# First chunk of x as float32 rows on the hardware queues, with w's first quarter behind them

## The chip, the cores and the metric

The kernel runs on one core of one Trainium2 chip. The metric is device time in microseconds of one execution. Time before: a median of 904.07 us over three runs (903.53 to 904.18).

## What is computed

```python
B, S, D = (16, 2048, 1024)          # x: (B, S, D), w: (D, D), decay: (D), all float32
xw = x @ w
out[:, 0, :] = xw[:, 0, :]
for t in range(1, S):
    out[:, t, :] = decay[None, :] * out[:, t - 1, :] + xw[:, t, :]
```

So it is one large matrix product and, along the time axis, a decayed running sum for each of the 1024 output columns.

## The kernel before, in words

The tokens are cut into 64 chunks of 512 (`TL`). The product is made transposed: weights stand still in TensorE as 64 tiles of 128 by 128 (`wsb`, index k for the eight slices of the inner dimension, n for the eight groups of output columns), and a chunk's tokens stream past as 512 columns. So x must arrive with its inner dimension on the partitions. In the steady state GpSimd's DMA queue loads a chunk with conversion to bf16 into `xb` (`load`, L105), one DMA for each quarter of the partitions ("quad"), VectorE transposes it in blocks of 32 (`turn`, L115, into `xw`), and a copy splits even and odd slices (`part`, L123, into `xt`). The other engines then form the running sums of each output group and store them through SP's queue (L306).

Everything that is issued is pinned: each engine executes its own instructions, DMA issues included, in the order in which the program text makes them. The table `agenda` writes that order out as letters; its entry -99 is the opening of the kernel, which is all that the change touches. The letters in it:

- `U0` to `U3` (`load_part`, L323): four DMAs each, a quarter of w: U0 is output half 0, even slices; U1 half 0, odd slices; U2 and U3 the same for half 1. They land in `stage` and are copied into `wsb` by `W`/`w` (`settle`, L330, VectorE/ScalarE; index 0 to 3 belongs to U0, 4 to 7 to U1, 8 to 11 to U2, 12 to 15 to U3) and by `q4`, `Q4` (L419).
- `M1`, `M2`, `M3` (`load_half`): four DMAs each for half a chunk of x: M1 is the second half of chunk 0, M2 and M3 are chunk 1.
- `I1`: GpSimd makes the bf16 identity `eye`.
- The first half of chunk 0 (256 tokens) goes another way: two DMAs (L341), one on SP's queue and one on ScalarE's, bring 128 float32 rows each. `H` (VectorE) and `J` (ScalarE) are `gather`, which converts and reorders rows (L376); `t` is `erect`, which transposes on TensorE against `eye` (L386); `O` (ScalarE) and `o` (VectorE) are `lay`, which copies the transposed block from PSUM into `xt` (L393). `gather`'s index i takes rows u = i mod 2, where u = 1 are the rows that ScalarE's queue brought.
- `K` (`spin_on`): ScalarE copies one column of a landed quad of U0 into a `gate` tile (L404), and two or three matmuls on that gate, whose result nobody reads, keep TensorE going. Twelve such matmuls on zeros (`spin`, L352) run at the very start.
- `E`, `F`, `G`: `turn` and `part` for one quarter of half a chunk (E4 to E7: second half of chunk 0; E8 to E15: chunk 1).
- `n` (`begin`): the first real matmuls, k even, n = 0 to 3, for the first (n0) and the second (n1) 256 tokens of chunk 0. After the agenda's opening, step 0 issues k odd for chunk 0, then chunk 1 in two halves. That finishes the first four output groups of two chunks.

ScalarE also issues DMAs: those of its own queue stand in its instruction order. Before the agenda it issues its one row DMA, then a copy called `touch` (L344). SP issues its row DMA and, after the spins, four small DMAs for `decay` (L356).

Of the kernel before, what the change touches and what calls it, by code (L numbers as in the profile page):

```python
# [9 lines left out]
FP32 = mybir.dt.float32  # L10
BF16 = mybir.dt.bfloat16
# [3 lines left out]
def _ap(ap_obj: bass.AP, new_ap, extra_offset=0):  # L15
    return dataclasses.replace(
        ap_obj,
        ap=[list(p) for p in new_ap],
        offset=ap_obj.offset + extra_offset,
    )  # L20
# [5 lines left out]
def kernel(  # L26
# [26 lines left out]
    nc = tc.nc  # L53
    pin = tc.keep_in_program_order
    B, S, D = x.shape
    assert w.shape == (D, D)

    NQ = 4
    P = 32
    CQ = D // NQ  # L60
    K = CQ // P
    M = K // 2
    TL = 512
    NJ = TL // P
    NC = S // TL
    R = K // 2
    CH = D // 2
    CR = CH // NQ

    const = ctx.enter_context(tc.tile_pool(name="const", bufs=1))  # L70
    sb = ctx.enter_context(tc.tile_pool(name="sb", bufs=1))
# [4 lines left out]
    def ring(pool, name, count, shape, dtype=FP32):  # L76
        i = turns[name] = turns.get(name, -1) + 1
        return pool.tile(shape, dtype, name=f"{name}{i % count}")

    def quad(q):  # L80
        return slice(q * P, (q + 1) * P)
# [12 lines left out]
    def ot_tile(nj):  # L94
        return ring(sb, "ot", 4, [128, nj, CR])

    xb_of = {}
    xw_of = {}
    xt_of = {}
# [25 lines left out]
    def matmul(ps, n, k, xt, t0=0, t1=TL, start=0, pairs=None):  # L125
        if pairs is None:
            rhs = xt[:, k // 2, k % 2, t0:t1]
        else:
            rhs = pairs[:, k // 2, t0 // P:t1 // P, :, k % 2].rearrange("p j i -> p (j i)")
        lhs = wsb[:, k, n].rearrange("p q i -> p (q i)")  # L130
        pin(nc.tensor.matmul(  # L131
            out=ps[:, t0:t1] if ps.shape[1] >= t1 else ps,
            lhsT=lhs,
            rhs=rhs,
            start=(k == 0 and t0 == start),
            stop=(k == K - 1),
        ))
# [3 lines left out]
    class Tile:  # L141
# [39 lines left out]
        def copy(self):  # L181
            self.xs = sb.tile([128, 2 * TL], FP32, name=f"xs{self.lot % 3}")[:, 0:self.T]
            parts = self.ps if isinstance(self.ps, tuple) else (self.ps,)
            size = self.T // len(parts)
            for i, ps in enumerate(parts):
                pin(nc.scalar.copy(out=self.xs[:, i * size:(i + 1) * size], in_=ps))  # L186
# [103 lines left out]
    class Outlet:  # L290
# [8 lines left out]
        def store(self, b, t0, j0, j1):  # L299
# [4 lines left out]
            for j in range(j0, j1, nj):  # L304
# [8 lines left out]

    room = [ot_tile(2 * NJ).rearrange("p j c -> p (j c)") for _ in range(2)]
    size = M * CH
    stage = {(0, 0): room[0][:, 0:size // 2].bitcast(BF16),
             (0, 1): room[0][:, size:size * 3 // 2].bitcast(BF16),
             (1, 0): room[1][:, 0:size // 2].bitcast(BF16),
             (1, 1): room[1][:, size // 2:size].bitcast(BF16)}

    def load_w(queues, h, e):
        for i, q in enumerate((0, 2, 1, 3)):
            pin(queues[i % len(queues)].dma_start(  # L323
                out=stage[h, e][quad(q)].rearrange("p (m d) -> p m d", m=M),
                in_=_ap(w, [[2 * D, P], [2 * P * D, M], [1, CH]],
                        (q * CQ + e) * D + h * CH)))

    def settle(h, e, m, copy):
        src = stage[h, e][:, m * CH:(m + 1) * CH]
# [3 lines left out]
    idle = const.tile([128, TL], BF16, name="idle")  # L333
    spare = ring(psp, "spare", 1, [128, TL])
    rows = const.tile([128, 2, P], FP32, name="rows")
    touch = const.tile([128, 1], BF16, name="touch")
    H = NJ // 2
    halves = ((0, H), (H, NJ))
    whole = room[1][:, size:2 * size].rearrange("p (u c) -> p u c", u=2)
    for u, queue in enumerate((nc.sync, nc.scalar)):  # L340
        pin(queue.dma_start(out=whole[:, u], in_=_ap(x, [[D, 128], [1, D]], u * 128 * D)))  # L341
    pin(nc.vector.memset(idle, 0.0))  # L342
    pin(nc.vector.memset(rows, 0.0))
    pin(nc.scalar.copy(out=touch, in_=idle[:, 0:1]))  # L344

    gates = [const.tile([128, 128], BF16, name=f"gate{q}") for q in range(NQ)]
    for gate in gates:
        pin(nc.vector.memset(gate, 0.0))

    def spin(count, by):  # L350
        for _ in range(count):
            pin(nc.tensor.matmul(out=spare, lhsT=by, rhs=idle, start=True, stop=True))  # L352

    spin(12, idle[:, 0:128])
    for q in range(NQ):
        pin(nc.sync.dma_start(  # L356
            out=rows[q * P:q * P + R],
            in_=_ap(decay, [[P, R], [CH, 2], [1, P]], q * CR)))
    cols = const.tile([128, 2, P], FP32, name="cols")

    def load_half(i):
# [5 lines left out]
    firsts = [ps[:, 0:TL] for ps in heads] + [spares[0]]  # L367
    seconds = [ps[:, TL:2 * TL] for ps in heads] + [spares[1]]
    eye = const.tile([128, 128], BF16, name="eye")

    upright = room[0][:, size * 3 // 2:2 * size].bitcast(BF16).rearrange(
        "p (e u m c) -> p e u m c", e=2, u=2, m=M)

    def gather(i, copy):
        e, u = i // 2, i % 2
        pin(copy(out=upright[:, e, u].rearrange("p m (q i) -> p m q i", q=NQ),  # L376
                 in_=whole[:, u].rearrange(
                     "p (q m i e) -> p e m q i", q=NQ, m=M, e=2)[:, e]))

    def bed(e):  # L380
        return seconds[e].bitcast(BF16).rearrange("p (m t) -> p m t", m=M)

    def erect(i):
        e, u = i // 2, i % 2
        for m in range(M):
            pin(nc.tensor.transpose(  # L386
                out=bed(e)[:, m, u * 128:(u + 1) * 128], in_=upright[:, e, u, m], identity=eye))

    def lay(i, copy):
        e, m = i // 2, i % 2 * 2  # L390
        if 0 not in xt_of:
            xt_of[0] = ring(sb, "xt", 5, [128, M, 2, TL], BF16)
        pin(copy(out=xt_of[0][:, m:m + 2, e, 0:H * P], in_=bed(e)[:, m:m + 2]))  # L393

    def begin(i):
        for k in range(0, K, 2):
            for n in range(R):
                if i == 0:
                    matmul(firsts[n], n, k, xt_of[0], 0, H * P)
                else:  # L400
                    matmul(firsts[n], n, k, xt_of[0], H * P, TL, pairs=xw_of[0])

    def spin_on(q):
        pin(nc.scalar.copy(out=gates[q][quad(q), 0:1], in_=stage[0, 0][quad(q), 0:1]))  # L404
        spin(3 if q == 0 else 2, gates[q])

    def load_part(i):
        load_w((nc.gpsimd,), i // 2, i % 2)

    def part_one(i, copy):  # L410
        part(i // 8, copy, i % 4, i % 4 + 1, *halves[i // 4 % 2])
# [106 lines left out]
    def turn_and_load(c):  # L518
# [16 lines left out]
        "w": lambda i: settle_one(i, nc.scalar.copy),  # L535
        "M": load_half,
        "U": load_part,
        "E": lambda i: turn(i // 8, *halves[i // 4 % 2], i % 4, i % 4 + 1),
        "F": lambda i: part_one(i, nc.vector.tensor_copy),
        "G": lambda i: part_one(i, nc.scalar.copy),  # L540
        "K": spin_on,
        "t": erect,
        "H": lambda i: gather(i, nc.vector.tensor_copy),
        "J": lambda i: gather(i, nc.scalar.copy),
        "O": lambda i: lay(i, nc.scalar.copy),
        "o": lambda i: lay(i, nc.vector.tensor_copy),
        "n": begin,
        "q": lambda i: settle_slots(i, 0, 1),
        "Q": lambda i: settle_slots(i, 1, R),
# [19 lines left out]
        "L": lambda i: load(*loads.pop(0)) if loads else None,  # L569
    }  # L570
    agenda = {
        -99: "U0 I1 M1 U1 M2 M3 U2 U3 H0 J1 t0 t1 H2 J3 t2 t3 O1 o0 K0 O3 o2 K2 K1 K3 W0 W1 w2 W3 n0 E4 E5 G4 E6 G5 E7 F6 G7 n1 q4 w5 Q4 W6 W7 D E8 E9 G8 E10 G9 E11 F10 G11 E12 L E13 G12 L E14 G13 E15 L F14 G15",
        0: "p0 z0 W8 W9 W10 W11",
        1: "g0",
        2: "L S1 L",
# [88 lines left out]
    for step, (g, n) in enumerate(slots):  # L664
        T = TL * len(g)
        left = step - len(slots)
        if n % R == 0:
            ns, nj = range(n, n + R), T // P
            if left == -2 * R:
                outlets = [Outlet(ns, H, half) for half in range(2)]  # L670
            else:
# [4 lines left out]
        if step == 0:  # L676
# [3 lines left out]
            for k0 in range(0, K, 2):  # L680
                for i in range(R):
                    for k in (k0, k0 + 1):
                        matmul(seconds[i], i, k, xt_of[1], 0, H * P,
                               pairs=xw_of[1] if k0 < 4 else None)
            for i in range(R):
                for k in range(K):
                    matmul(seconds[i], i, k, xt_of[1], H * P, TL, H * P,
                           pairs=xw_of[1] if i < 2 else None)
        if step < R:
            ps = heads[n] if n < 3 else tuple(spares)  # L690
        else:
# [16 lines left out]
            elif step == K:  # L708
                todo = []
                nexts = (ring(psp, "spare", 1, [128, TL]), ring(psp, "ps", 3, [128, TL]))  # L710
                for l in range(len(g)):
                    for i, half in enumerate((ps[:, l * TL:(l + 1) * TL], nexts[l])):
                        for k in range(K):
                            matmul(half, n + i, k, xt_of.get(g[l]),
                                   pairs=xw_of[g[l]] if g[l] in (3,) else None)
# [51 lines left out]
```

## Time and profile before

| what | value |
|---|---|
| median of three runs | 904.07 us |
| the profiled execution | 903.72 us, of which the span of the trace is 901.9 us |
| TensorE (PE) busy | 891.2 us, 99% of the span |
| VectorE (DVE), ScalarE (ACT), GpSimd (POOL) busy | 91%, 76%, 73% |
| first real matmul starts | 9.95 us |
| first group of four output blocks done, next one starts | 25.55 us |
| mean granted TensorE clock | 1.000 of full speed |

Times in a profile line are in microseconds from the start of the span: first the start, then the duration, the engine, the source line, what is written from what, and how many instructions were merged into the row; in brackets the idle time of that engine before the row and what ended it. ACTq and SPq are DMA issues of ScalarE and SyncE.

### The profile page before, as it was taken

To read this page: it belongs to the slowest core of one execution; us is meant where nothing else is said; L and a number is where in the kernel's file an instruction comes from. 1 tells how busy PE (TensorE), PEld (TensorE's weight loads), DVE (VectorE), ACT (ScalarE), POOL (GpSimd) and SP (SyncE) were. 2 spreads that over 40 slices of the span, in tenths; PEclk is the share of its full clock that TensorE was granted. 3 is DMA by queue.
4 is the path that set the end of the run, shared out by engine and by line. 5 is a ranking of instruction groups with operands and counts; after the bars stand their busy time and mean duration, and the time that the engine had idled before them with its cause. 6 is when DMAs were issued, how large, how long until landed. Compare 5 with 4: busy or idle time off the path is not lost.

```text
span 901.9 us, 12229 instructions
## 1 busy us (share of the span) xinstructions
PE 891.2 (99%) x4131; PEld 411.9 (46%) x4213; DVE 823.5 (91%) x636; ACT 687.1 (76%) x962; POOL 657.2 (73%) x757
## 2 busy tenths in 40 slices
PE   8999999999999999999999999999999999999998
PEld 5544444444444444444444444444444444444444
DVE  4999998989999999999998999999999999999998
ACT  4889867778877877878778778777787787787743
POOL 8888678768767768677677687777777776876532
PEclk9999999999999999999999999999999999999999
DMA  9999999999999999999999999999999999999868
GB/s 193 195 215 218 229 212 207 216 233 247 247 248 255 248 255 252 246 254 250 222 235 228 218 236 227 233 226 227 232 230 227 227 236 222 226 228 221 177 153 231
DMA packets 402382, 204.77 MB, mean 227 GB/s; under 512 B 9360, under 2 KB 401552, under 8 KB 402320
## 3 DMA queue, kind: packets, MB, share of 16 engines
q1 hardware_dynamic: 265664, 134.77, 60.8%
q0 software_dynamic: 136512, 68.70, 56.8%
q8 instruction: 33, 0.54, 0.2%
q10 hardware_dynamic: 144, 0.52, 0.1%
q14 instruction: 29, 0.24, 0.1%
HBM read 138.42 MB, written 134.22 MB: 302 GB/s over the span
## 4 chain that ended last, share of the span: by engine, by line
PE 97%; DMA 1%; issue 1%; POOL 0%; DVE 0%; ACT 0%; DVEq 0%; POOLq 0%
PE ps L131 96%; PE spare L131 1%; DMA ot<-in_w_dram 1%; POOL ot L323 0%; DVE so L233 0%; PE ps L460 0%; PE spare L460 0%; ACT xb L467 0%; DVE wsb L419 0%; DVEq L419 0%; POOLq L751 0%
## 5 line engine op out<-in xcount | busy, mean ns | idle before, releaser
L131 PE MATMUL ps<-xt,wsb 128*128 128x512 bf16 (+1 forms) x3946 | 862.6, 378 | 4.7 <-DVE wsb L419 0.4
L131 PEld LDWEIGHTS <-wsb 128*128 128x128 bf16 x4160 | 406.5, 98 | 479.8 <-issue 0.9
L208 POOL TENSOR_TENSOR xs<-h,xs 128x512 f32<-128x512 f32 (+1 forms) x190 | 242.7, 1278 | 184.1 <-ACT h L169 83.1
L283 DVE STREAM_TRANSPOSE ot<-so 128x1024 f32<-128x1024 f32 (+2 forms) x265 | 300.2, 1171 | 6.5 <-DMA out_dram<-ot 4.4
L186 ACT COPY xs<-ps 128x1024 f32<-128x1024 f32 (+1 forms) x190 | 188.8, 994 | 149.3 <-PE ps L131 137.5
L266 POOL TENSOR_TENSOR so<-h,xs 128x512 f32<-128x512 f32 (+1 forms) x190 | 241.2, 1271 | 46.9 <-ACT h L169 27.2
L123 ACT COPY xt<-xw 128x2048 bf16<-128x2048 bf16 (+1 forms) x133 | 240.6, 1816 | 9.5 <-DVE xw L115 9.5
L105 POOL DMA_DIRECT2D xb<-in_x_dram x260 | 171.6, 661 | 2.9 <-DMA ot<-in_w_dram 0.9
L169 ACT ACTIVATE h<-so,dec 128x512 f32<-128x512 f32 (+1 forms) x190 | 145.3, 766 | 32.8 <-DVE so L213 29.9
L115 DVE STREAM_TRANSPOSE xw<-xb 128x2048 f32<-128x2048 f32 (+1 forms) x74 | 145.9, 1981 | 6.5 <-DMA xb<-in_x_dram 6.5
L213 DVE TENSOR_TENSOR_SCAN so<-spare,keep,xs 128x512 f32<-128x512 f32 (+1 forms) x97 | 119.8, 1237 | 25.9 <-POOL xs L208 25.6
L213 DVE TENSOR_TENSOR_SCAN so<-spare,xs 128x512 f32<-128x512 f32 x93 | 113.0, 1217 | 25.4 <-POOL xs L208 22.8
L169 ACT ACTIVATE h<-ps,dec 128x512 f32<-128x512 f32 (+1 forms) x189 | 129.3, 684 | 0.0
L233 DVE TENSOR_TENSOR_SCAN so<-dec,ps 128x1024 f32<-128x1024 f32 x34 | 76.9, 2260 | 0.8 <-ACT h L169 0.6
L233 DVE TENSOR_TENSOR_SCAN so<-dec,keep,ps 128x1024 f32<-128x1024 f32 (+2 forms) x35 | 74.7, 2138 | 0.0
L270 ACT COPY keep<-so 128x1 f32<-128x1 f32 x136 | 25.2, 188 | 9.1 <-DVE so L233 8.7
L204 ACT COPY so<-keep 128x1 f32<-128x1 f32 x97 | 18.4, 191 | 2.6 <-DVE ot L283 2.4
L131 PE MATMUL spare<-xt,wsb 128*128 128x512 bf16 (+1 forms) x68 | 14.0, 329 | 0.0
L323 POOL DMA_DIRECT2D ot<-in_w_dram x16 | 9.0, 561 | 2.9 <-POOLq L751 0.9
L202 POOL MEMSET so<- 128x1 f32 x93 | 10.7, 116 | 0.6 <-DVE ot L283 0.6
L131 PE MATMUL ps<-xw,wsb 128*128 128x256 bf16 (+1 forms) x56 | 9.3, 307 | 0.8 <-DVE xw L115 0.8
L352 PE MATMUL spare<-idle 128*128 128x512 bf16 x12 | 5.3, 632 | 1.2 <-DVE idle L342 1.2
(46 smaller groups left out, 43.9 us busy)
## 6 DMA issues: line engine op xcount, KB each, us to landing
out_dram<-ot SPq DMA_DIRECT2D x236, 512.0 KB, 10.8
xb<-in_x_dram POOLq DMA_DIRECT2D x248, 256.0 KB, 7.8
out_dram<-ot SPq DMA_DIRECT2D x56, 128.0 KB, 2.5
ot<-in_w_dram POOLq DMA_DIRECT2D x16, 128.0 KB, 5.6
out_dram<-ot SPq DMA_DIRECT2D x8, 256.0 KB, 4.2
xb<-in_x_dram POOLq DMA_DIRECT2D x12, 128.0 KB, 5.3
out_dram<-xb SPq DMA_DIRECT2D x4, 256.0 KB
ot<-in_x_dram ACTq DMA_DIRECT2D x1, 512.0 KB, 4.9
```

The lines of the kernel that those rows point to most:

```text
L105: pin(nc.gpsimd.dma_start(out=xb_of[c][quad(q), j0:j1], in_=_ap(x, [[D, P], [P * D, j1 - j0], [1, CQ]], (b * S + t0 + j0 * P) * D + q * CQ)))
L115: pin(nc.vector.transpose(out=dst.rearrange("p (m j i) -> p j m i", m=M, i=P)[:, j0:j1, m0:m1], in_=src.rearrange("p (j m c) -> p j m c", ...
L123: pin(copy(out=xt_of[c][:, m0:m1, :, j0 * P:j1 * P], in_=src))
L131: pin(nc.tensor.matmul(out=ps[:, t0:t1] if ps.shape[1] >= t1 else ps, lhsT=lhs, rhs=rhs, start=(k == 0 and t0 == start), stop=(k == K - 1),))
L169: pin(nc.scalar.activation(out=h, in_=src, func=mybir.ActivationFunctionType.Copy, scale=dec[:, self.n:self.n + 1]))
L186: pin(nc.scalar.copy(out=self.xs[:, i * size:(i + 1) * size], in_=ps))
L208: pin(nc.gpsimd.tensor_tensor(out=odds, in0=self.g, in1=odds, op=ALU.add))
L213: pin(nc.vector.tensor_tensor_scan(out=so[:, 3:T + 2:2], data0=squares[-1][:, n:n + 1].to_broadcast([128, T // 2]), data1=self.xs[:, 1:T:2 ...
L233: pin(nc.vector.tensor_tensor_scan(out=so[:, t + 2:t + 2 + size], data0=dec[:, n:n + 1].to_broadcast([128, size]), data1=ps, initial=befor ...
L266: pin(nc.gpsimd.tensor_tensor(out=self.so[:, 2:T + 2:2], in0=self.h, in1=self.xs[:, 0:T:2], op=ALU.add))
L270: pin(nc.scalar.copy(out=self.keep, in_=self.so[:, self.T + 1:self.T + 2]))
L283: pin(nc.vector.transpose(out=outlet.ot[:, j:j + size, c0:c0 + P], in_=self.so[:, t1:t1 + size * P].rearrange("p (i t) -> p i t", t=P)))
```

## The change

The second 256 tokens of chunk 0 also come as float32 rows, two more DMAs on SP's and ScalarE's queues, and take the way over `gather`, `erect` and `lay`. w's first quarter (before: U0 on GpSimd, converted on the way) now comes as float32 behind those rows, cut in two along the slices m and by quads: SP takes quads 0 and 2, ScalarE quads 1 and 3, two DMAs each per cut. In program order that makes six DMAs on SP (then the four of `decay`) and six on ScalarE, where `load_rest(nc.scalar, 1)`, five DMAs, stands after `touch` and before every gather. GpSimd no longer issues U0 and M1; it first makes `eye`, then executes `hold`, a copy of one column of the first 256 rows, so that it waits for them, and then issues U1, M2, M3, U2, U3. The gates go; `K5` and `K1` are plain spins of five and one. `begin` runs 512 columns at a time, one k per letter. The staging for the new rows is `xb`'s buffer of chunk 0, and the converted rows stand in `xw`'s.

```diff
-    def load_w(queues, h, e):
-        for i, q in enumerate((0, 2, 1, 3)):
-            pin(queues[i % len(queues)].dma_start(
...
+    def load_w(queue, h, e, m0=0, m1=M, quads=range(NQ)):
+        for q in quads:
+            pin(queue.dma_start(
...
-    for u, queue in enumerate((nc.sync, nc.scalar)):
-        pin(queue.dma_start(out=whole[:, u], in_=_ap(x, [[D, 128], [1, D]], u * 128 * D)))
+    def load_rest(queue, u):
+        load_rows(queue, 1, u)
+        for m0, m1 in ((0, 2), (2, M)):
+            load_w(queue, 0, 0, m0, m1, (u, u + 2))
+
+    load_rows(nc.sync, 0, 0)
+    load_rows(nc.scalar, 0, 1)
+    load_rest(nc.sync, 0)
     pin(nc.vector.memset(idle, 0.0))
     pin(nc.vector.memset(rows, 0.0))
     pin(nc.scalar.copy(out=touch, in_=idle[:, 0:1]))
...
+    load_rest(nc.scalar, 1)
...
     def begin(i):
-        for k in range(0, K, 2):
-            for n in range(R):
-                if i == 0:
-                    matmul(firsts[n], n, k, xt_of[0], 0, H * P)
-                else:
-                    matmul(firsts[n], n, k, xt_of[0], H * P, TL, pairs=xw_of[0])
...
+        for n in range(R):
+            matmul(firsts[n], n, 2 * i, xt_of[0])
+
+    def hold(i):
+        pin(nc.gpsimd.tensor_copy(out=held, in_=wholes[0][:, :, 0:1].rearrange("p u c -> p (u c)")))
...
-        -99: "U0 I1 M1 U1 M2 M3 U2 U3 H0 J1 t0 t1 H2 J3 t2 t3 O1 o0 K0 O3 o2 K2 K1 K3 W0 W1 w2 W3 n0 E4 E5 G4 E6 G5 E7 F6 G7 n1 q4 w5 Q4 W6 W7 D E8 ...",
+        -99: "I1 v U1 M2 M3 U2 U3 H0 J1 t0 t1 H2 J3 t2 t3 O1 o0 O3 o2 K5 H4 J5 t4 t5 H6 J7 t6 t7 o4 O5 K1 W0 n0 o6 w1 n1 W2 O7 n2 W3 n3 q4 w5 Q4 W6 W7 D E8 ...",
```

## The prediction

> **What bounds the kernel now.** I read the chain of waits on the page first, then TensorE's rows of the timeline, then the rows of the other engines for the first 28 us, then the chain of that stretch.
>
> ```profile
> PE 97%; DMA 1%; issue 1%; POOL 0%; DVE 0%; ACT 0%; DVEq 0%; POOLq 0%
> ```
>
> That is the chain of the whole span; these are TensorE's own rows of the timeline:
>
> ```profile
> 9.95 0.49 PE L131 MATMUL ps<-xt,wsb 128*128 128x256 bf16 x3
> ...
> 12.62 0.51 PE L131 MATMUL ps<-xw,wsb 128*128 128x256 bf16 x3 [0.76 <-DVE xw L115]
> ...
> 14.97 0.82 PE L131 MATMUL ps<-xt,wsb 128*128 128x512 bf16 x2 [0.37 <-DVE wsb L419]
> ...
> 25.55 14.66 PE L131 MATMUL ps<-xt,wsb 128*128 128x512 bf16 x65
> ```
>
> From 14.97 us TensorE runs without a hole to the tail, so whatever moves the end of the first group (25.55) moves the end of the kernel by as much. A 512-column matmul is issued every 0.216 us, a 256-column one every 0.109 us. The first group is 16 x 0.216 (n0 and n1 together) + 10.45 (step 0, measured from 14.97, with 0.13 of slack) = 13.9 us; from 9.95 that would end at 23.9. The other 1.7 us are the two holes before 12.62 and 14.97 (waits for the second half of chunk 0, then for U1). So a perfect opening that starts at S ends the group at S + 13.9, and breaks even at S = 11.65.
>
> **What the change does to S if all goes as drawn.** ScalarE and the DMA queues:
>
> ```profile
> 0.74 0.41 ACTq L341 DMA_DIRECT2D ot<-in_x_dram  x1
> 0.75 0.39 SPq L341 DMA_DIRECT2D ot<-in_x_dram  x1
> ...
> 5.43 0.80 DVE L376 CAST ot<-ot 128x512 bf16<-128x512 f32 x2 [3.92 <-DMA ot<-in_x_dram]
> 5.65 1.21 ACT L376 CAST ot<-ot 128x512 bf16<-128x512 f32 x2 [2.98 <-DMA ot<-in_x_dram]
> 7.23 0.58 ACT L393 COPY xt<-ps 128x512 bf16<-128x512 bf16 x1 [0.37 <-PE ps L386]
> ...
> 7.84 0.98 DVE L393 COPY xt<-ps 128x512 bf16<-128x512 bf16 x2 [1.62 <-ACT xt L393]
> ```
>
> The DMA view of the first 26 us shows 365 to 416 GB/s while both queues bring rows; 1.05 MB more take 2.6 us, so rows 256 to 511 land near 8.1, w's first half (0.52 MB) near 9.4, the second near 10.7. H4 stands behind o2, though, and o0 and o2 wait for ScalarE's O1 and O3 (last row: done at 8.82). So H4 (0.40) ends near 9.2, H6 at 9.6, the transposes of H4 and J5 (0.22 for four at full clock) near 9.8, o4 (0.49) near 10.4, W0 from float32 (0.40, like the cast) near 10.8: S = 10.8. w1, W2 and W3 then stay ahead of 0.86 us of matmuls per k. U1, now behind `hold`, has the queue from about 5.9; the 4.2 MB up to its end land near 13.3 at that rate, its copies end before n3 does (14.25). End 10.8 + 13.9 = 24.7, a gain of 0.85 us: 903.2.
>
> Sizes off the path: GpSimd loses eight issues (2.32 + 2.41) and waits until 5.7 instead; behind `hold` are U1, M2, M3, U2, U3 and all later loads. M2 (VectorE took it at 17.49) follows the same 5 MB as before and is needed 0.6 us before step 0's second part, M3 (20.21) later still, U2 (23.75) at the end of the group; none is late here, and less so if S is late. VectorE loses 1.42 + 0.38, gains 0.80 + 0.98; ScalarE loses 1.66 + 0.80, gains 1.21 + 1.15; SP has nothing else to do until 38.45. Those are cover, not path; without it the largest of them is 0.98.
>
> **The step that I think decides.** ScalarE now issues five more DMAs, and its first cast J1 stands behind them in its order. An issue alone is cheap (0.41, so 2.67 + 5 x 0.41 = 4.7, before 5.65). But an issue can wait. On GpSimd it does:
>
> ```profile
> 1.31 1.25 POOL ot L323 x2
> 2.56 5.65 DMA ot<-in_w_dram
> 8.21 0.28 issue
> 8.50 0.54 POOL ot L323
> ```
>
> This is the chain of the opening. The third DMA is issued at 2.56 and lands at 8.21; the eleventh, eight later, is issued 0.28 us after that. The records of the trace name the semaphore of each DMA: eight on GpSimd (99 to 106), in turn, and each issue waits for the landing of the DMA eight before it. The hardware queues' records, in order of time:
>
> ```
> 0.74 ACT  semaphore=107          38.45 SP  semaphore=117
> 0.75 SP   semaphore=109          38.82 SP  semaphore=118
> 1.24 SP   semaphore=112          39.44 SP  $S[107]>= semaphore=107
> 1.62 .. 2.26 SP  113, 114, 115   45.16 SP  $S[109]>= semaphore=109
> ```
>
> Eight again, shared by SP and ScalarE: the ninth DMA takes 107, which was ScalarE's, and waits for it. Before, only six are issued in the opening and nothing is felt. The change has sixteen. In program order: rows 0 (SP), rows 1 (ScalarE), five of SP, five of ScalarE, four of decay. ScalarE's last four are the ninth to twelfth: they wait for rows 0 (5.4), rows 1 (5.6), SP's second rows (8.1) and SP's first piece of w. That last landing: two pieces of 131 KB in parallel take 0.65 us at 405 GB/s; at the rate at which GpSimd's quads land (131 KB each 0.66 us) 1.3 us. So 8.7 to 9.4; I take 9.1, the middle, since quads 0 and 1 share their stretch with GpSimd's U1. With the issue's 0.4, J1 starts at 9.5 instead of 5.65. If records are given out in another order than the program's (107 went to ScalarE, though SP's row stands first), decay or ScalarE come earlier or later; the last of ScalarE's five then waits for something that lands between 5.6 and 9.4.
>
> From J1 on the chain is the same as drawn above, where J1 at 5.65 gave 10.8: J1, J3, O1, O3 on ScalarE, then o2, H4, H6, o4, W0 on VectorE. So n0 starts at J1 + 5.15 = 14.65. By then w, U1 and M2 have landed, and w1, W2, W3, q4, W6 are ahead of the matmuls. End of the group 14.65 + 13.9 = 28.55: **+3.0 us**. Bounds: J1 at 8.4 (ScalarE waits only for SP's second rows) gives +1.9; J1 at 10, with the rest of ScalarE's chain stretched by 0.5, gives +4.0.
>
> The sum against the profiled execution: span 901.9 + 3.0 = 904.9, with 1.8 us around it 906.7. That execution (903.72) lay 0.35 below the median, to which I add: 904.07 + 3.0 = 907.1.
>
> **Rivals.**
> 1. *The issues don't hold ScalarE up* (the semaphores fall so that ScalarE's wait for the first rows at most, or are already passed): S = 10.8, 903.2. For it: nothing before shows ScalarE held by an issue. Against: the wait is in the records of SP and GpSimd alike. The point that decides: break-even is J1 = 6.5 (11.65 - 5.15), so a wait beyond the first rows' landing turns the gain into a loss.
> 2. *Not held up, but w lands slowly*: its pieces go to 32 partitions each, as GpSimd's quads do, and those never exceed some 200 GB/s written. Then 1.05 MB take 5.3 us from 8.1: W2 at 13.9, n2 and n3 end near 15.9, the group at 26.3, +0.8: 904.8. Against: those quads are converted, so 400 GB/s are read at that rate, and either side could be the limit. [...]
> 3. *Held up, and the clock falls.* TensorE then has nothing from about 6.7 (t0) to 10.2 (t1):
>
> ```profile
> 1.20 5.30 PE L352 MATMUL spare<-idle 128*128 128x512 bf16 x12 [1.20 <-DVE idle L342]
> ```
>
> and by stretches of the tail (length, busy time of the five engines, then PEclk, DMA share, GB/s):
>
> ```profile
> 901.00:902.00 1.00, 0.00 (x0) 0.00 (x0) 0.00 (x0) 0.00 (x0) 0.00 (x0) 0.59 0.00 0
> ```
>
> The early spins take 0.43 us each, twice the later 0.216; and in the last microsecond, some 3 us after the last matmul, the granted clock (0.59) goes down. A pause of 3.5 us may do the same here: K5 then takes 2.1 instead of 1.1 and holds t4 back by 0.8, t4 and t5 cost 0.4 more, and n0 to n3, if still slow, up to 3.4. I take +1.2 to +3.4 on top: 908.3 to 910.5. [...]
>
> **How the numbers follow.** Held up at full clock 0.46, held up with the clock down 0.24, as drawn 0.20, slow w 0.10. A measurement of this kernel tells about 0.2%, 1.8 us. Slower by more than that takes J1 past 8.3: nearly all of the first two, 0.65. Within: the last two and the early end of the first, 0.32. A gain of 1.8 would need S = 9.85, before o4 has ended: 0.03. The likeliest case's own range is 906.0 to 908.1; that of 8 in 10 reaches down to the case as drawn and up into the slow clock: 903.0 to 909.5.
>
> **What would show it.** Right: in the timeline ScalarE's issues between 2.7 and 9, with gaps, J1 near 9.5 with the DMA named before it; `hold` near 5.7 on GpSimd; t0 alone on TensorE before 7 and t1 after 10; n0 near 14.6 with no holes after; the 512-column row of step 4 starting near 28.5. Clock: K5's spins at 0.43 each. Wrong: J1 at 5.65 and n0 near 10.8 (then rival 1; with W2 waiting for a DMA, rival 2), or holes in TensorE after n3, which would mean that GpSimd's late start is felt after all.

## The result, and the profile after

The changed kernel takes **906.54 us** (median of seven runs, 906.25 to 907.19), the kernel before 903.66 (903.53 to 904.18) beside it: 2.9 us more, a ratio of 1.0031 (95% interval 1.002 to 1.0043). The profiled execution of the changed kernel took 907.0, with a span of 905.2; before it was 903.72 with 901.9.

The chain of waits still belongs to TensorE:

```profile
PE 98%; DMA 1%; ACT 0%; DVE 0%; ACTq 0%; issue 0%
```

So the 3.3 us of span must be looked for in the opening. These are rows of the timeline of the changed kernel, ScalarE's and its queue's first, then VectorE's, GpSimd's and TensorE's (start and length in us; in brackets the idle time before, and what ended it):

```profile
1.66 1.12 ACTq L323 DMA_DIRECT2D ot<-in_w_dram  x2
...
5.54 3.38 ACTq L323 DMA_DIRECT2D ot<-in_w_dram  x2
8.96 1.19 ACT L391 CAST xw<-ot 128x512 bf16<-128x512 f32 x2 [6.29 <-DMA xb<-in_x_dram]
...
5.54 0.76 DVE L391 CAST xw<-ot 128x512 bf16<-128x512 f32 x2 [4.33 <-DMA ot<-in_x_dram]
...
5.75 0.27 POOL L417 COPY held<-ot 128x2 f32<-128x2 f32 x1 [4.43 <-DMA ot<-in_x_dram]
6.28 2.33 POOL L323 DMA_DIRECT2D ot<-in_w_dram  x4 [0.27 <-issue]
...
6.03 0.40 PE L401 MATMUL ps<-eye,xw 128*128 128x128 bf16 x4 [0.53 <-DVE xw L391]
9.66 1.46 PE L401 MATMUL ps<-eye,xw 128*128 128x128 bf16 x12 [3.23 <-ACT xw L391]
10.91 2.34 PE L366 MATMUL spare<-idle 128*128 128x512 bf16 x5
...
14.96 0.82 PE L131 MATMUL ps<-xt,wsb 128*128 128x512 bf16 x3
...
29.00 3.18 PE L131 MATMUL ps<-xt,wsb 128*128 128x512 bf16 x14
```

VectorE casts its half of the first rows (H0) at 5.54, as soon as they land (5.52). ScalarE's half landed at 5.69, but J1 starts only at 8.96: ScalarE issued two of its four pieces of w at 1.66, and the other two took from 5.54 to 8.92. Its cast used `ot`, and yet the wait that ended is named as one for `xb`, the second rows: the wait of an issue, not of the cast. TensorE has t0 at 6.03, then nothing for 3.23 us until t1. From 14.96 there is no hole, and the group ends at 29.00, 3.45 later than before. The chain of waits of the first 30 us goes the same way, through the second rows' transfer, ScalarE's last issue, J1 and t1 (start, length, what):

```profile
1.25 7.34 DMA xb<-in_x_dram
...
8.60 0.32 ACTq L323
...
8.96 0.65 ACT xw L391
...
9.66 1.46 PE ps L401 x12
```

What the issues waited for stands in the records of the trace, in order of time (number of the semaphore that each DMA will raise, and waits):

```
0.74 ACT 100   0.75 SP 102   1.19 SP 105   1.25 ACT 106   (rows)
1.66 SP 107    1.66 ACT 108  2.12 SP 109   2.15 ACT 110   (w)
5.54 ACT waits for 102   5.71 SP waits for 100   8.14 SP waits for 105   8.60 ACT waits for 106
```

Eight semaphores, and the ninth to twelfth DMA each wait for one of the four transfers of rows. ScalarE's last waits for 106: its own second rows, landed at 8.58.

The same execution by stretches (length; then the busy time of TensorE, its weight loads, VectorE, ScalarE and GpSimd; then granted clock, DMA share, GB/s):

```profile
4.34:7.75 3.41, 1.55 (x10) 0.52 (x7) 0.76 (x2) 0.00 (x0) 1.73 (x4) 1.00 1.01 411
7.75:11.16 3.41, 1.50 (x13) 1.41 (x14) 0.24 (x1) 1.77 (x4) 3.14 (x6) 0.50 1.10 251
11.16:14.58 3.42, 3.42 (x20) 2.14 (x19) 1.72 (x6) 1.69 (x3) 1.25 (x3) 0.50 1.26 234
14.58:17.99 3.41, 3.41 (x19) 1.51 (x18) 3.15 (x13) 2.21 (x5) 2.88 (x6) 1.00 1.45 194
```

The granted clock was half from 7.75 to 14.58, so K5's five spins at 10.91 were issued every 0.43 us instead of 0.216. And the DMA queues, which moved 411 GB/s while rows came (4.34 to 7.75), moved 251 after that (7.75 to 11.16).

### The profile page after: what moved, and what is told of

It is laid out like the page before. It is cut to its first block, busy times and chain, and to the rows that moved or that the text cites. A ratio compares the mean times of both kernels' runs of the same rounds, so it can differ in the third digit from the quotient of the medians.

```text
span 905.2 us, 12303 instructions
## 1 busy us (share of the span) xinstructions
PE 896.7 (99%) x4210; PEld 412.4 (46%) x4210; DVE 824.2 (91%) x631; ACT 686.9 (76%) x959; POOL 652.6 (72%) x750
## 4 chain that ended last, share of the span: by engine, by line
PE 98%; DMA 1%; ACT 0%; DVE 0%; ACTq 0%; issue 0%
PE ps L131 96%; PE spare L131 1%; DMA xb<-in_x_dram 1%; PE spare L366 0%; PE ps L401 0%; DVE so L233 0%; PE spare L401 0%; ACT xw L391 0%; PE ps L472 0%; PE spare L472 0%; ACTq L348 0%; ACT xb L479 0%; ACTq L323 0%; ACT L361 0%
## 5 line engine op out<-in xcount | busy, mean ns | idle before, releaser
L131 PE MATMUL ps<-xt,wsb 128*128 128x512 bf16 x4028 | 868.3, 378 | 0.0
L105 POOL DMA_DIRECT2D xb<-in_x_dram x256 | 169.2, 662 | 4.9 <-DMA ot<-in_w_dram 3.3
L204 ACT COPY so<-keep 128x1 f32<-128x1 f32 x97 | 18.4, 191 | 2.4 <-DVE ot L283 2.2
L202 POOL MEMSET so<- 128x1 f32 x93 | 10.7, 117 | 0.3 <-DVE ot L283 0.3
L131 PE MATMUL ps<-xw,wsb 128*128 128x256 bf16 (+1 forms) x44 | 7.4, 315 | 0.0
L323 POOL DMA_DIRECT2D ot<-in_w_dram x12 | 6.7, 565 | 0.6 <-issue 0.5
```

Of the source, the lines that this page charges most:

```text
L105: pin(nc.gpsimd.dma_start(out=xb_of[c][quad(q), j0:j1], in_=_ap(x, [[D, P], [P * D, j1 - j0], [1, CQ]], (b * S + t0 + j0 * P) * D + q * CQ)))
L131: pin(nc.tensor.matmul(out=ps[:, t0:t1] if ps.shape[1] >= t1 else ps, lhsT=lhs, rhs=rhs, start=(k == 0 and t0 == start), stop=(k == K - 1),))
```

## The experiments

Edits are against the changed kernel unless said otherwise; "n0" is the start of the first product matmul, "end" the start of step 4's 512-column row, both of the profiled execution. Each time is set against the kernel before, run on the same chip (medians 903.66 to 903.97). Behind each expectation stands the result: the median in us, the lowest and highest run, then the ratio to the kernel before with its 95% interval.

| kernel | J1 | n0 | end | end against 25.55 | time against before |
|---|---|---|---|---|---|
| changed | 8.96 | 14.96 | 29.00 | +3.45 | +2.9 |
| e1, ScalarE's second cut later | 5.65 | 13.38 | 28.71 | +3.16 | +2.8 |
| e2, one cut | 5.78 | 14.16 | 29.89 | +4.34 | +4.2 |
| e3, pause filled | 9.14 | 13.73 | 27.77 | +2.22 | +1.9 |
| e4, before with ScalarE held | 9.46 | (other order) | 29.83 | +4.28 | +2.9 |
| e5, one cut by halves | 5.72 | 11.86 | 25.90 | +0.35 | +0.5 |
| e6, second cut on SP | 5.67 | 10.66 | 27.51 | +1.96 | +1.8 |
| e7, e6 without GpSimd's hold | 5.72 | 12.18 | 27.83 | +2.28 | +1.8 |
| e8, w on SP alone | 5.85 | 13.63 | 27.67 | +2.12 | +3.6 |
| e9, four transfers by k | 6.18 | 18.25 | 40.76 | +15.2 | +15.0 |
| e10, e9 and U1 by k too | 6.05 | 17.62 | 38.67 | +13.1 | +12.8 |
| e11, e6 with GpSimd's hold later | 5.66 | 10.65 | 26.77 | +1.22 | +1.4 |

That the end of the first group sets the time holds in every row to about 0.5 us but e4 and e8, whose profiled runs were the slowest and the fastest of five.

**Is it the hold on ScalarE?** e1 takes the two issues that wait out of J1's way:

```diff
-    load_rest(nc.scalar, 1)
+    load_rest(nc.scalar, 1, ((0, 2),))      # second cut: a letter "l" in the agenda
-  ... O1 o0 O3 o2 K5 ...
+  ... O1 o0 O3 l o2 K5 ...
```

> The change, with ScalarE's last two DMAs of w issued behind O3 instead of ahead of J1; same DMAs, same queues. Theory A (ScalarE's casts stand behind issues that wait for a semaphore of an earlier DMA): J1 starts near 5.7 instead of 8.96, TensorE never pauses 3 us, and what is left is the slow landing of w (its first cut lands at 9.5 to 10.9 in the changed kernel): n0 near 11.4, end of the group 25.3, 903.4 us. Theory B (w's own landing, last piece at 14.7, sets the pace and J1's delay lies beside it): n2 still waits for that landing near 15, some 906 us.

906.71 (906.62 to 907.49), 1.0034 [1.0022, 1.0046]. ScalarE's and TensorE's rows of e1:

```profile
5.65 1.21 ACT L391 CAST xw<-ot 128x512 bf16<-128x512 f32 x2 [2.98 <-DMA ot<-in_x_dram]
...
8.81 2.16 ACTq L323 DMA_DIRECT2D ot<-in_w_dram  x2
11.01 1.19 ACT L391 CAST xw<-xb 128x512 bf16<-128x512 f32 x2 [3.07 <-DMA ot<-in_w_dram]
...
16.40 0.82 PE L131 MATMUL ps<-xt,wsb 128*128 128x512 bf16 x3 [0.49 <-DVE wsb L331]
```

J1 is at 5.65, as it should be without the wait. But the wait moved: the second of the two issues now waits for a piece of w (landed at 10.63), and J5 behind it starts at 11.01. The piece issued then lands at 15.79, and TensorE waits for it; its clock was half from 11.25 to 14.66, over the start of the products. So the time is that of the changed kernel, not the 903.4 of theory A, and e1 does not tell what J1's wait alone costs: undoing one hold bought another.

e4 does the opposite: the kernel before, whose transfers are untouched, with one copy on ScalarE ahead of J1 that waits for U0's last quad.

```diff
-  U0 I1 M1 U1 M2 M3 U2 U3 H0 J1 t0 ...
+  U0 I1 M1 U1 M2 M3 U2 U3 v H0 J1 t0 ...   # v: ScalarE copies a column of stage's quad 3
```

> The kernel before, with one more copy on ScalarE ahead of J1, of one column of the last landed quad of U0, so that ScalarE is held until that lands (8.9); nothing else of the change. Theory A: J1 near 9.1 instead of 5.65, n0 near 13.4 instead of 9.95, the later holes are filled by the delay, the group ends near 27.3 instead of 25.55, 905.5 us, up to 906 with the clock down. If ScalarE's delay is covered by the loads of the opening (theory B): no more than 904 us.

906.79 (906.15 to 907.99), 1.0035 [1.0022, 1.0048]: more than expected. Its rows:

```profile
9.46 1.19 ACT L376 CAST ot<-ot 128x512 bf16<-128x512 f32 x2
...
11.52 4.02 PE L352 MATMUL spare<-idle,gate 128*128 128x512 bf16 x9
```

J1 at 9.46, and nine spins in 4.02 us, 0.43 and more each: the clock was half from 9.23 to 16.06 here too. So holding ScalarE alone, with nothing of the change in the kernel, costs what the change costs. A hold of this length is enough for the loss. It is not proof that it is all of the loss in the changed kernel: there the last piece of w landed at 14.71, and where it lands at 14.59 with ScalarE free (e6, below) the group still ends at 27.51, 1.96 of the 3.45 us late.

**Does a ninth DMA wait, or do five issues take long?** e2 issues w's quads uncut: eight DMAs ahead of the decays, four on each queue, with three more than before still ahead of J1 on ScalarE.

```diff
-        for m0, m1 in ((0, 2), (2, M)):
+        for m0, m1 in ((0, M),):
```

> The change, with w's first quarter not cut in two: four DMAs instead of eight, so that rows and w take eight semaphores and no issue of ScalarE finds one in use. Theory A: J1 near 5.7 although all five issues still stand ahead of it; n0 has to wait for the whole quarter, near 12, so S = 12.4 and 904.4 us. If the issues were slow in themselves, or the queue full (rival: a queue that takes only so many bytes), ScalarE would be held as in the changed kernel, J1 near 8.5 to 9, and the time near 906.5 us. Theory B gives 906 as well, since w lands no earlier.

908.08 (907.76 to 908.33), 1.0046 [1.0034, 1.0059].

```profile
5.78 1.21 ACT L391 CAST xw<-ot 128x512 bf16<-128x512 f32 x2 [3.11 <-DMA ot<-in_x_dram]
...
14.16 1.16 PE L131 MATMUL ps<-xt,wsb 128*128 128x512 bf16 x3 [3.71 <-DVE wsb L331]
```

J1 at 5.78, right behind its rows, which landed at 5.76: the issues ahead of it, all among the first eight DMAs, cost it nothing. The ninth, SP's first of decay, is the one that waits: with the same eight ahead of it in e5, below, SP is done issuing w at 2.71 and issues it at 5.78. But n0 stands at 14.16 instead of near 12, waiting 3.71 us for w, and in this pause the clock fell, so that n0 to n3 ran at half of it (columns as above):

```profile
14.51:17.93 3.42, 3.42 (x10) 1.22 (x8) 2.22 (x9) 1.17 (x2) 3.22 (x7) 0.50 1.43 193
```

The group takes 15.73 us from n0 here, 14.04 where the clock stays up. The prediction's second rival, w landing slowly, was real, and hidden in the changed kernel behind ScalarE.

**Why does w land slowly?** In e2 SP brings quads 0 and 2, ScalarE 1 and 3, so that two quads that are neighbours are written at the same time. e5 gives SP 0 and 1, ScalarE 2 and 3:

```diff
-            load_w(queue, 0, 0, m0, m1, (u, u + 2))        # both with ((0, M),)
+            load_w(queue, 0, 0, m0, m1, (2 * u, 2 * u + 1))
```

> The uncut version (four DMAs for w, no issue waits), with the quads dealt out differently: SP brings 0 and 1, ScalarE 2 and 3, so that the two queues write to partitions of different halves at any time; before, quad 0 beside quad 1, then 2 beside 3. Uncut, w's 1.05 MB took from 7.3 to 13.6 us. Theory P (partitions 32 apart share a way into the memory): w lands near 10.3, n0 near 11.2, the group ends near 25.1, 903.5 us. Theory Q (pieces of 32 partitions or rows of 2 KB are slow on these queues whatever their neighbours): w lands near 13.6 as before, 908 us.

904.3 (903.83 to 905.69), 1.0006 [0.9997, 1.0015]: 3.8 us less than e2 for the same bytes in the same number of transfers (n0 2.30 us earlier, the other 1.69 from the half clock in e2), though w landed later than the 10.3 expected. The stretch 8.5 to 10 us of e2, then of e5 (columns as above):

```profile
8.50:10.00 1.50, 0.91 (x13) 0.68 (x12) 0.83 (x4) 1.22 (x2) 1.50 (x4) 1.00 1.01 220
```

```profile
8.50:10.00 1.50, 1.07 (x16) 0.93 (x17) 1.06 (x3) 1.20 (x2) 1.50 (x4) 1.00 1.05 371
```

220 against 371 GB/s. The last quad lands at 13.56 in e2 and at 11.26 in e5, and n0 there is the end of the wait for it:

```profile
11.86 0.82 PE L131 MATMUL ps<-xt,wsb 128*128 128x512 bf16 x3 [1.71 <-DVE wsb L331]
...
25.90 15.74 PE L131 MATMUL ps<-xt,wsb 128*128 128x512 bf16 x70
```

What the runs show of theory P is these two rates: 220 GB/s where the two queues write quads 32 partitions apart, 371 where they write quads 64 apart. The shared way into the memory, theory P's cause, is not shown.

e8 takes ScalarE's queue out: SP brings all of w, a quad at a time, in the order 0, 2, 1, 3.

> The change with ScalarE issuing rows only and SP all of w, uncut, quads in the order 0, 2, 1, 3, one behind the other. Theory P with one queue that keeps its order: neighbours lie in different halves, but one piece at a time fills only half of the ways: 1.05 MB at some 210 GB/s from 7.6 to 12.6, n0 near 13, 905.2 us. If two queues at once are what slows the pieces (theory R, whatever the partitions), w lands near 10.4 and the time is near 903.5 us. Theory Q: w near 13.6, 908 us.

907.34 (905.88 to 907.42), 1.0034 [1.0022, 1.0047]. The four quads land at 9.8, 10.9, 12.0 and 13.0, one each 1.1 us, 236 GB/s for 262 KB: a single stream of quads is about as fast as two on neighbours (220 in e2), and of these three only the two streams 64 partitions apart were faster (371 in e5). By itself e8 would also fit a limit of one queue, which no run here tests apart. n0 is at 13.63 and the end at 27.67, which gives +2.1, the time of the profiled run (905.88); the other four took about 907.3 (expected: 905.2). Their mean granted clock is 0.997 to 0.998, against 0.999 in the profiled run. One more stretch of 3.41 us at half clock would take some 0.002 off the mean and, with TensorE busy, cost 1.7 us (an estimate from these lengths), so their 1.4 us more are probably the clock's; only the profiled run has a trace, so this is not shown.

**What did the half clock cost?** e3 fills TensorE's pause with 15 spins between t0 and t1:

```diff
-  ... H0 J1 t0 t1 H2 ...
+  ... H0 J1 t0 K15 t1 H2 ...
```

> The change, with fifteen unread matmuls on zeros put between t0 and t1, where TensorE paused from 6.4 to 9.7. ScalarE stays held up. Theory A with a small price for the clock: the granted clock stays at full speed, K5 takes 1.1 instead of 2.3 us, t4 starts behind H4 (12.6 instead of 13.05), n0 near 14.2 instead of 14.96, and the time falls by 0.8 to 905.7 us. Theory C (the pause and the half clock are most of the loss): 904.5 us or less. If the clock costs nothing: 906.5 us.

905.76 (905.46 to 906.15), 1.002 [1.0011, 1.0029]: 0.8 us less than the changed kernel (1.0 when each is set against its own runs of the kernel before). Two stretches of e3 (columns as above):

```profile
4.16:7.57 3.41, 2.98 (x17) 1.32 (x16) 0.76 (x2) 0.00 (x0) 1.85 (x4) 1.00 1.02 412
7.57:10.98 3.41, 3.04 (x23) 1.57 (x22) 0.09 (x1) 1.84 (x4) 3.15 (x6) 1.00 1.08 257
```

TensorE is busy for 2.98 of 3.41 us where it had 1.55, and the clock stays full; K5 then takes 1.24 instead of 2.34, and n0 comes 4.59 after J1 instead of 6.00.

**And if nothing is held, does the drawn 903.2 come out?** e6 holds ScalarE nowhere and deals the quads out by halves of the partitions: ScalarE brings two quads of the first cut, SP the other two, and SP, which has nothing else to do, issues the whole second cut, where it may wait.

```diff
-        for m0, m1 in ((0, 2), (2, M)):
-            load_w(queue, 0, 0, m0, m1, (u, u + 2))
+        load_w(queue, 0, 0, 0, 2, (2 * u, 2 * u + 1))
     ...
     load_rest(nc.scalar, 1)
+    load_w(nc.sync, 0, 0, 2, M, (0, 2, 1, 3))
```

> The change with both mended: quads dealt out by halves as in the last kernel, w cut in two again, and ScalarE issuing only its rows and the first cut of quads 2 and 3 (eight DMAs in all up to there), while SP, which nothing waits for, issues the second cut of all four quads and takes the waits. Theories A and P: J1 at 5.7, first cut near 9.0, second near 10.8, n0 near 10.8, no hole up to U1: 903.1 us, 0.8 below the kernel before. With theory Q instead of P: first cut near 10.8, second near 14, W2 then holds TensorE up at n2: 905 to 906 us.

905.63 (904.9 to 907.71), 1.0027 [1.0018, 1.0036]: a miss by 2.5 us. TensorE's rows:

```profile
10.66 0.82 PE L131 MATMUL ps<-xt,wsb 128*128 128x512 bf16 x3 [0.55 <-DVE wsb L331]
...
15.20 0.82 PE L131 MATMUL ps<-xt,wsb 128*128 128x512 bf16 x3 [2.63 <-DVE wsb L331]
```

n0 came as drawn, at 10.66, but after two k steps TensorE waits 2.63 us for the second cut. SP's last two transfers were issued at 8.10 and 8.45 and landed at 13.80 and 14.59; in between, from 9.62, GpSimd's queue moved U1. e7 takes `v` out of the agenda, e11 moves it to the second rows:

```diff
-  in_=wholes[0][:, :, 0:1]...      # e11: GpSimd waits for rows 256 to 511
+  in_=wholes[1][:, :, 0:1]...
```

> The last kernel without GpSimd's wait for the first 256 rows: U1's issues start near 1.3 instead of 6.2. If GpSimd's packets are only served once the hardware queues run dry, as the first packets at 10.1 (changed kernel, issued 6.3) and 4.9 (kernel before, issued 1.3) suggest, nothing moves by more than 0.3 us: U1 lands as before. If they are served in turn, U1 takes its share from 3 us on, rows and w land up to 2.5 us later, and the time rises by 1 to 2 us.

> The kernel that brings the first cut of w by halves of the partitions and the second cut by SP alone, with GpSimd's hold on rows 256 to 511 (landed near 8.4) instead of rows 0 to 255 (5.6). There, SP's last two transfers of the second cut were issued at 8.10 and 8.45, had their first packet only at 11.4, when GpSimd's had been flowing since 9.6, and landed at 13.8 and 14.6: TensorE waited 2.6 us. Theory T (GpSimd's transfers, issued earlier, took the stretch that those two should have had): now GpSimd issues its first at 8.7 or later, behind SP's last; the second cut lands by 12, the hole of 2.6 goes, n0 stays near 10.7; the second quarter lands some 1 us later than the 14.8 it had, so a new hole of 0.5 to 1.5 us stands after n3; group end 25.2 to 26.2, time 903.5 to 904.5, against 905.6. Rival (a hardware transfer that is issued after the first queueing is slow by itself, some 5 us from issue to landing): it lands at 13.3 to 14.5 all the same, the hole stays above 2 us, and the second quarter comes later still: 905.6 to 907.

e7: 905.59 (905.2 to 906.05), 1.0019 [1.0011, 1.0028], the time of e6, as expected. The way there was not: GpSimd's first packet moved at 5.62, among the rows, and the second rows landed about 0.9 later (8.89 and 9.44, against 8.08 and 8.43); n0 came at 12.18 and the hole after it was 1.44 instead of 2.63. What was expected of its packets was wrong; leaving out the hold on the first rows moves bytes from one wait to another and is worth nothing (905.59 against 905.63).

e11: 905.11 (904.88 to 907.3), 1.0018 [1.0009, 1.0027].

```profile
9.08 2.33 POOL L323 DMA_DIRECT2D ot<-in_w_dram  x4 [0.30 <-issue]
...
10.65 0.82 PE L131 MATMUL ps<-xt,wsb 128*128 128x512 bf16 x3 [0.39 <-DVE wsb L331]
...
16.18 0.82 PE L131 MATMUL ps<-xt,wsb 128*128 128x512 bf16 x3 [1.91 <-DVE wsb L431]
```

The last two transfers of the second cut now land at 11.34 and 11.74, 2.5 and 2.9 us earlier, and the hole behind n1 is gone: GpSimd's transfers had taken its stretch. The wait came back for U1 (L431 is its first copy), which landed at 15.81 and is needed near 14.1; at 1.91 the hole is larger than the 0.5 to 1.5 expected, and the time misses the expected 903.5 to 904.5. From 11.74 to 15.15 all queues together moved only 137 GB/s; why, these runs do not show. What is gained in one transfer turns up as a wait for another: whichever of the three queues is late, TensorE waits for it (2.63 us for w in e6, 1.91 for U1 in e11).

**Fewer, wider transfers.** e9 brings w in four transfers, one for each k step, over all 128 partitions; e10 does so with U1 as well.

```diff
-        for m0, m1 in ((0, 2), (2, M)):
-            load_w(queue, 0, 0, m0, m1, (u, u + 2))
+        for m in (u, u + 2):
+            pin(queue.dma_start(
+                out=stage[0, 0][:, m * CH:(m + 1) * CH],
+                in_=_ap(w, [[CQ * D, NQ], [2 * D, P], [1, CH]], 2 * P * m * D)))
```

> The changed kernel, with w's first quarter brought in four transfers instead of eight, one for each of its four k steps, over all 128 partitions (262 KB each); SP brings steps 0 and 2, ScalarE steps 1 and 3, so each queue has four transfers in all and the eight semaphores suffice. Theory P (the wait for a ninth semaphore and the narrow transfers, which share a way in, are the two costs): J1 near 5.7, the four transfers land between 9.4 and 11.0 in the order in which they are needed, n0 starts near 10.7 as in the kernel with the second cut on SP, no hole of 2.6 us after it; the group ends near 24.7 and the time is 903.0 (902.6 to 903.5), below the kernel before. Rival (packets of 2 KB are slow whatever the partitions, some 235 GB/s as in the changed kernel): the first two land near 10.7, the last two near 13; n0 near 11.2, a hole of 0.3 to 0.6 us at the third step, 903.8 to 904.4.

> As the kernel sent with it, and GpSimd too brings w's second quarter by k steps over all partitions, four transfers of 262 KB read, each. If the second quarter is in time in the one (landed before n3 has ended, near 14.1), nothing changes: 903.0. If TensorE waits for it there after n3, this one gives back that wait, up to 0.5 us, since the first of the four lands first and is all that the next step needs.

Far off on both theories: e9 918.93 (917.19 to 919.87), 1.0163 [1.0148, 1.0178], and e10 916.74 (915.81 to 916.91), 1.0137 [1.012, 1.0154]. TensorE in e9:

```profile
18.25 1.46 PE L131 MATMUL ps<-xt,wsb 128*128 128x512 bf16 x3 [7.20 <-DVE wsb L331]
...
25.61 1.46 PE L131 MATMUL ps<-xt,wsb 128*128 128x512 bf16 x3 [4.05 <-DVE wsb L331]
```

From 8.5 to 10 us the two hardware queues together moved 24 packets in each 0.5 us, most at 84 ns (in the changed kernel 106 in the 0.5 us from 7.5, at a median of 84 ns): 24 x 84 = 2.0 us of packets in 0.5, the work of four of the 16 DMA engines that the page counts. What held both queues to that, the runs do not show. Nor did the ninth's wait go: the decays, issued at 3.27 and after, took up the semaphores, and ScalarE's second transfer of w waited until 5.59.

No version beats the kernel before; e5 equals it.

## Why the prediction was right, step by step

- **What bounds the kernel: right.** The end of the first group set the time, without holes after n0. The group took 14.04 us from n0 in the changed kernel, in e3, e5 and e8 alike, where 13.9 was forecast.
- **"The step that I think decides": right, with another wait in it.** Eight semaphores, the ninth to twelfth DMA wait, and ScalarE stands still behind them; without the ninth J1 is at 5.78 (e2), and holding ScalarE alone costs 2.9 us (e4). The chain of waits runs through J1, but close beside it lay another: "By then w, U1 and M2 have landed" holds for w alone (14.71, n0 at 14.96); U1 landed at 15.30, M2 at 17.28, both in time. What the hold by itself adds to that is small here: e6, with ScalarE free and w's second cut about as late, ends at 27.51, and e3, with ScalarE held and the clock up, at 27.77. Of the 3.45 us, some 2 would have stayed (an estimate from e6, whose quads are paired otherwise); the rest is mostly the half clock that the hold brought. ScalarE's last did not wait for SP's first piece of w, though, but for its own second rows: semaphores went out in order of issue (100 ScalarE, 102 and 105 SP, 106 ScalarE, then 107 to 110 in turn), not in the program's. J1 came at 8.96 instead of 9.5, near the "J1 at 8.4" of the lower bound.
- **n0 = J1 + 5.15: the size was off.** At full clock it is 4.59 (e3): o2 ends 2.73 after J1 there, 3.17 in the kernel before, from which the 5.15 was read, and the rest takes 1.86 instead of 1.98. At the half clock of the changed kernel it is 6.00.
- **Rival 3, the clock falls: it happened, at a lower price than its +1.2 to +3.4** (its own terms, 0.8, 0.4 and up to 3.4, add up to 1.2 to 4.6). The profile shows it, and filling the pause wins back 0.8 us in the medians (e3). n0 to n3 were not slowed, because the clock rose at 14.58, 0.38 ahead of n0. The event belonged to this rival; the time, 906.54, fell into the likeliest case's own range.
- **The sum.** Forecast 9.5 + 5.15 + 13.9 = 28.55. Measured 8.96 + 6.00 + 14.04 = 29.00. A wait 0.54 shorter, a chain 0.56 shorter, a clock that cost 1.41 of it in this execution and a group 0.14 longer add up to +0.45. The size was hit partly because errors of both signs met. With the clock kept up (e3) the likeliest case itself comes to 905.8, below its own range of 906.0 to 908.1; the half clock, which belongs to rival 3, brought the time back into it. That is luck.
- **The case as drawn, 903.2: its S was right, its landings wrong.** With nothing held, n0 came at 10.66 (e6) and 10.65 (e11), where 10.8 was forecast. The step that failed is "at 405 GB/s" for all that comes behind the rows: that is about the rate at which rows over 128 partitions came (411 from 4.34 to 7.75 in the changed kernel). w's quads, paired as in the change, came at 220 to 250, and with the pairs mended, the transfers behind the first cut were still slower than drawn (209 GB/s from 9.88 to 13.30 in e6). The second cut, forecast for 10.7, landed at 11.74 (e11) to 14.59 (e6), and U1, for 13.3, at 14.8 (e6) to 15.8 (e11). So rival 1's 903.2 was too low: its nearest tests, e5, e6, e7 and e11, gave 904.3 to 905.6. Rival 2, with its 200 GB/s, had the better reason, and its 904.8 was low too: with the quads paired as in the changed kernel and ScalarE not held it came to 908.1 (e2), of which 1.7 are the half clock, and n0 there waits for the whole quarter, not for a first cut.
- **GpSimd's hold "late for none": right here**, because n0 is so late: U1 landed at 15.30, needed near 18.4. With n0 at 10.65 it was late by 1.91 (e11).

## What to carry to other kernels

Count the DMAs that an engine has issued ahead of its first piece of work, over all engines that share the completion semaphores (eight here, for SP and ScalarE). In the changed kernel ScalarE's two issues beyond them went out only when older transfers had landed (at 5.54 and 8.60, behind landings at 5.52 and 8.58), and J1 stood behind them until 8.96 instead of 5.65. Such an issue belongs on an engine with no work of its own, as on SP in e6, where J1 started at 5.67. Price a transfer from rows of its own shape and partitions: two queues that write neighbouring quads moved 220 GB/s where two that write quads 64 partitions apart moved 371. And when one wait is taken away, look which transfer is late next before counting the gain.

## What the runs showed of the hardware beyond that

- The granted clock changed at times that lie 3.41 us or twice that apart, at another offset in each run (down and up again at 7.75 and 14.58 in the changed kernel, 11.25 and 14.66 in e1, 14.51 and 17.93 in e2, 9.23 and 16.06 in e4), and a pause did not need to be complete. It fell at the end of stretches of 3.41 us in which TensorE was busy for 1.55 (the changed kernel), 0.95 (e1), 0.80 (e4) and 0.34 us (e2), and did not after 1.70 (e5) and 1.51 (e6) nor, in the profiled run, after 1.44 (e8): the two kinds overlap between 1.44 and 1.55 us, and what decides there these runs do not show. Runs of one kernel differ in it: six of e6 at a mean clock of 0.999 to 1.0 took 904.9 to 905.63 us, the other five at 0.997 to 0.998 took 906.96 to 907.71; in e1 runs at 1.0 took 906.67 and 906.73 us and those at 0.997 and 0.998 906.62 to 907.49, in e7 those at 0.999 and 1.0 905.2 to 906.05 and those at 0.997 and 0.998 905.5 to 906.02.
- GpSimd's first packet moved 3.4 to 5.3 us after its first issue in most runs, with rows or w still coming on the hardware queues (issued 1.31 and moved 4.88 before; 6.28 and 10.13 in the changed kernel; 6.36 and 11.68 in e2), and 1.6 to 1.7 us after it in e11 (9.08 and 10.64, when SP's queue alone was moving w, since ScalarE's pieces had landed by 10.10) and in e9 (6.33 and 8.04, in a stretch, 7.49 to 10.90, in which all queues together moved 157 GB/s). What decides, these runs do not show: in e8 SP's queue alone was moving from 8.8 on, and the first packet still came only at 11.36 (issued 6.42).
- Where its packets started to flow behind such an issue, a transfer on a hardware queue was late in its turn: 6.1 us from issue to landing in the changed kernel (8.60 to 14.71) and in e6 (8.45 to 14.59), against 3.4 in e11 (8.38 to 11.74), where GpSimd issued later.
